# A hybrid recurrent decoder layer in fp32: the low half of each weight unit kept in HBM after its first use

## The chip, the cores and the metric

The kernel runs on one core of one Trainium2 chip. The metric is the device time of one execution in microseconds (us), lower is better. TensorE is called PE, VectorE DVE, ScalarE ACT and GpSimd POOL, as in the profile; SP is the engine whose queue issues every DMA of this kernel.

## The reference, cut to what matters

One layer over a prompt of 2048 tokens and 8 x 4 sample tokens, width 1024. The four weight matrices are multiplied with all tokens; between the first and the second stand four recurrent mixers that work through the tokens in chunks.

```python
u = x @ w_in                       # 1024 -> 3860, split among mixers A, B, C, D
y = concat(A(u), B(u), C(u), D(u)) # gated DeltaNet, Mamba-2 SSD, HGRN2, mLSTM: causal, with a state
h = LayerNorm(alpha * x + y @ w_out)
x = LayerNorm(alpha * h + relu(h @ w_up)**2 @ w_down)   # 1024 -> 4096 -> 1024
```

## The kernel before

The tokens are cut into NB = 4 blocks of 512; the 32 sample tokens ride along with block 0 in the projection and with block 2 behind it (544 columns then, in two pieces). Blocks 0 to 3 go through the projection (`do_P`, 31 column tiles of `w_in`), then each block through `w_out` (`do_W`) and the feed-forward part (`do_F`). The mixers run beside this as streams ("ma" for A, "mb" for B, C and D).

Every product is made in three passes to keep fp32 accuracy: a weight and an activation are each split into a high part, rounded to the matmul's format, and a low part, the rest; then hi x hi, lo x hi and hi x lo are accumulated in PSUM. A *unit* of weights is 1024 (or, for `w_dn`, 512) rows by 128 columns and is streamed in halves of [128, 4, 128] floats, 256 KB. The list `units` holds all 832 halves in the order of their use: 248 of `w_in` (62, four times), 64 of `w_out`, 256 of `w_up` and 264 of `w_dn`. 206 of them are distinct.

- `w_get(i)` loads half i into a `wraw` buffer (four of them).
- `w_split()` makes `whi` (ACT, sometimes DVE: `cpv`) and `wlo` = `wraw` - `whi` (`tt` on POOL or DVE, as `tvp` chooses). Four buffers each.
- `gemm` calls `w_pump()` ahead of half `cur`; the pump loads up to half cur+4 and splits up to half cur+2. A half is 4 x 3 matmuls, or twice as many for 544 columns.
- `w_first` and `w_rest` do the split of the first four halves in two steps.

The order on each engine is the order in which the program is written out. A planner (`_Run`) sets it: it carries a clock per engine with rough costs, and after each k step of a product (`R.tick()`) lets those steps of the mixers, evacuations and norms through whose inputs should be ready. `tvp` asks the same clocks whether POOL or DVE would be done first. So a step that is taken out of the program moves the place of others. All instructions run in order on their engine; SP's queue is one such order, for loads, stores and the mixers' transfers alike. Nearly all engine calls pass through one helper line (253), and all DMAs but a few through line 374, so the names of the tiles tell the instructions apart: `pd` is a product's PSUM tile, `g` an activation, `nb<-ud32d` a broadcast that the DeltaNet solve reads back from HBM, `UA` to `UD` the projected activations in HBM, `hTd` the normed input there.

Of the kernel before, what the change touches and what calls it, by code (L numbers as in the profile page):

```python
# [10 lines left out]
F32 = mybir.dt.float32  # L11
# [32 lines left out]
LATE_W = 5.0  # L44
# [262 lines left out]
def _dve_cost(fn, n, out, k):  # L307
    if fn in ("bn_stats", "tensor_reduce"):
        n = 1
        for x in k["in_"].shape[1:]:  # L310
            n *= x
    per = {"reciprocal": 0.00625, "tensor_tensor_scan": 0.00195, "tensor_copy": 0.00053}.get(fn, 0.00106)
    if fn == "tensor_scalar" and _sb(k["in0"]):
        per = 0.00053
    if fn == "bn_aggr":
        return 0.13
    return 0.06 + n * per + 0.06 * _ptrs(k, ("scalar", "scalar1", "scalar2"))
# [6 lines left out]
def _pool_cost(fn, n, out, k):  # L324
    return 0.25 + n * {"tensor_tensor": 0.00214, "tensor_scalar": 0.0012, "tensor_copy": 0.0036}.get(fn, 0.001)
# [20 lines left out]
def kernel(ctx: ExitStack, tc: tile.TileContext, t):  # L346
# [17 lines left out]
    drp = ctx.enter_context(tc.tile_pool(name="drp", bufs=1, space=DRAM))  # L364
# [5 lines left out]
    mult, add, sub = ALU.mult, ALU.add, ALU.subtract  # L370
    vmax, vmin = ALU.max, ALU.min

    def dma(out, in_):
        nc.sync.dma_start(out=out, in_=in_)
        R.cost("dma", 0.55, 2.5)
# [13 lines left out]
    def tt(out, a, b, op, eng=None):  # L389
        (eng or V).tensor_tensor(out=out, in0=a, in1=b, op=op)  # L390
# [10 lines left out]
    def tvp(n, late=0.0):  # L401
        now = max(R.clock["pe"], R.cur.ready)
        v = max(R.clock["dve"], now) + _dve_cost("tensor_tensor", n, None, {})
        g = max(R.clock["pool"], now) + _pool_cost("tensor_tensor", n, None, {})
        return G if g < max(v, R.clock["pe"] + late) else V

    def cpv(out, in_, n, late=0.0):
        now = max(R.clock["pe"], R.cur.ready)
        if max(R.clock["act"], now) + _act_cost("", n, None, {}) <= max(max(R.clock["dve"], now) + _dve_cost("tensor_copy", n, None, {}), R.clock["pe"] + late):
            cp(out, in_)  # L410
        else:
            V.tensor_copy(out, in_)
# [110 lines left out]
    units = []  # L523
    wst = {"nload": 0, "nsplit": 0, "cur": 0, "turn": 0}
    raws, his = {}, {}

    def w_get(i):
        w = sb4.tile([128, 4, 128], F32, tag="wraw", name="wraw")
        dma(w, units[i])
        raws[i] = w  # L530

    def w_pump():
        cur = wst["cur"]
        while wst["nload"] < min(cur + 5, len(units)):
            i = wst["nload"]
            w_get(i)
            wst["nload"] += 1
            if wst["nsplit"] < min(cur + 3, wst["nload"]):
                w_split()
        while wst["nsplit"] < min(cur + 3, len(units)):  # L540
            w_split()

    def w_split():
        i = wst["nsplit"]
        w = raws.pop(i)
        hi = sb4.tile([128, 4, 128], F32R, tag="whi", name="whi")
        lo = sb4.tile([128, 4, 128], F32R, tag="wlo", name="wlo")
        cpv(hi, w, 512, LATE_W - 1.0)
        tt(lo, w, hi.bitcast(F32), sub, tvp(512, LATE_W))
        his[i] = (hi, lo)  # L550
        wst["nsplit"] += 1

# [5 lines left out]

    def w_rest(i, eng):
        hi, lo = his[i]  # L560
        tt(lo, raws.pop(i), hi.bitcast(F32), sub, eng)

    def pieces(nt):
        if nt <= 512:
# [73 lines left out]
    def split_next(key):  # L638
        if not pend[key]:
            return  # L640
        k, st, nt = pend[key].popleft()
        XS[key].append(split_kt(st, k, nt))

    def queue_set(key, tiles, nt):
        pend[key] = deque((k, x, nt) for k, x in enumerate(tiles))
        XS[key] = []

    def fin_set(key):
        R.until(lambda: key in pend)
        while pend[key]:  # L650
            split_next(key)
        return XS.pop(key)
# [18 lines left out]
    def ln0_start():  # L671
# [5 lines left out]
        for src, n in tiles:  # L677
            x = [g2(), g2()]
            for half in range(2):
                dma(x[half][:n, 0:512], src[:, half * 512:half * 512 + 512])  # L680
            xs.append(x)
        w_get(0)
        dma(con, t["consts"])
        w_get(2)
        dma(par, t["params"])
        w_get(1)
# [11 lines left out]
        for i, half, e in ((1, 0, "a"), (2, 0, "g"), (4, 0, "v"), (3, 0, "a"), (0, 0, "g"), (0, 1, "v"), (4, 1, "v"), (1, 1, "a"), (2, 1, "g"), (3, 1, "v")):  # L698
# [5 lines left out]
            else:  # L704
                ts(xv, xv, r_, mult, m_, add, G if e == "g" else V)
        w_first(2)
        w_rest(0, G)
        w_rest(2, V)
        xs = xs[1:] + xs[:1]
        px = psa.tile([128, 512], F32, tag="a", name="pa_")  # L710
# [7 lines left out]
        def first(k):  # L718
            if k in (0, 1):
                w_first(2 * k + 1)  # L720
                w_rest(2 * k + 1, G)
            xh, xl = XS["P", 0][k]
            for u in range(2):
                hi, lo = his[2 * u + k // 4]
                seq = ((hi, xh), (lo, xh), (hi, xl))
                for n, (w, x) in enumerate(seq):
                    for p, c0, cn in psu[u]:
                        mm(p[:, 0:cn], w[:, k % 4, :], x[:, c0:c0 + cn], start=k == 0 and n == 0, stop=k == 7 and n == 2)

        for k in range(8):  # L730
# [17 lines left out]
            if k == 5:  # L748
                for i in range(4, 8):
                    w_get(i)  # L750
                wst["nload"] = 8
        w_split()
        w_split()
        setup()
# [48 lines left out]
    def y_pre(b):  # L803
# [5 lines left out]
        for k in range(8):  # L809
            st.append(load_kt(yTd[b], yTx, k, nt))  # L810
            yield
        queue_set(("W", b), st, nt)
        for k in range(EARLY_W):
            split_next(("W", b))
            yield
# [941 lines left out]
    def do_P(b, xs, nt):  # L1757
        for u in range(2 if b == 0 else 0, NPU):
            if b == NB - 1 and u == W0_AT:
                do_W(0, fin_set(("W", 0)), f_nt(0))  # L1760
                XS["F", 0] = {}
# [10 lines left out]
    def do_W(b, xs, nt):  # L1772
        acc = accs[b] = []
        st = deque(load_kt(hTd[b], hTx, d, nt) for d in range(2))
        for d in range(8):
            if d + 2 < 8:
                st.append(load_kt(hTd[b], hTx, d + 2, nt))
            ps = pieces(nt)
            gemm(ps, xs)
            acc.append(g2())  # L1780
            R.start(w_evac(ps, nt, acc[d], st.popleft()))
# [178 lines left out]
    def f_nt(b):  # L1960
        return NTM if b == FDEC else TB

    def do_F(b):
# [10 lines left out]
        for c in range(FFB):  # L1974
# [9 lines left out]
            elif b + 1 < NB:  # L1984
                do_W(b + 1, fin_set(("W", b + 1)), f_nt(b + 1))
                XS["F", b + 1] = {}
# [30 lines left out]
            del r2[c]  # L2017

    def fill_units():
        W = lambda: [units.extend([t["w_out_u"][d, 0], t["w_out_u"][d, 1]]) for d in range(8)]  # L2020
        for b in range(NB):
            for u in range(NPU):
                if b == NB - 1 and u == W0_AT:
                    W()
                units.extend([t["w_in_u"][u, 0], t["w_in_u"][u, 1]])
        for b in range(NB):
            f = 0
            for c in range(FFB):
                for j in range((4 if c == 0 else 3) + (1 if c + 1 < FFB else 0)):
                    units.extend([t["w_up_u"][f, 0], t["w_up_u"][f, 1]])  # L2030
                    f += 1
                if c == FFB - 1 and b + 1 < NB:
                    W()
                for q in range(2 if b == NB - 1 and c == FFB - 1 else 1):
                    units.extend(t["w_dn_u"][c, d] for d in range(8))

    fill_units()
    ln0_start()
    dma(lng, t["ln2_g"].partition_broadcast(128))
# [126 lines left out]
```

## Time and profile before

| | |
|---|---|
| median of 3 runs | 3067.88 us (3064.59 to 3075.63) |
| profiled execution | 3071.5 us, span 3069.7 us |
| busy: PE, DVE, ACT, POOL | 2897.1, 2156.1, 1244.2, 1632.5 us |
| granted TensorE clock, mean | 0.983 |
| DMA | 404.04 MB on SP's queue, 46.3% of the 16 DMA engines' time |

The span runs from the first to the last instruction. "Busy" counts an engine's own work, not waits. A row of a group gives the engine, the operation, out<-in, the count, then busy time and mean ns of one, then the idle time just ahead of it with what ended it. A row of waits gives total, number and longest. The stages by time: the projections of the four blocks up to about 1050 us, block 0's `w_out` inside their end; then `do_F` of block 0 up to about 1600, of blocks 1 to 3 up to the end. The mixers run from about 200 to 2420 us.

### The profile page before, as it was taken

Reading aid. Unit: us, or ns where it says so; the run is one execution under the profiler, and the core shown is the slowest. Engines: PE = TensorE matmul, PEld = TensorE weight load, DVE = VectorE, ACT = ScalarE, POOL = GpSimd, SP = SyncE. Lnnn points to the kernel's source line nnn. Section 1 sums busy time; section 2 is a strip of 40 time slices with the busy share of each in tenths; the row PEclk is TensorE's granted clock in tenths of the full one; section 3 lists DMA queues with packets and bytes.
Section 4 is the critical chain, followed back from the end, with each engine's and each line's share of the span. In section 5 each row is a group of like instructions: output and inputs, shape, how many; then the busy total and the mean of one; then the engine's idle time right before and its main releaser. Section 6 shows DMA issues by size and latency. Waiting matters only on the chain. (4 is left out here: it accounts for less than half of the span.)

```text
span 3069.7 us, 48033 instructions
## 1 busy us (share of the span) xinstructions
PE 2897.1 (94%) x16668; PEld 2479.8 (81%) x16668; DVE 2156.1 (70%) x4077; ACT 1244.2 (41%) x2653; POOL 1632.5 (53%) x1982
## 2 busy tenths in 40 slices
PE   7889899998999899999999999999999999999997
PEld 7778767777877778888787877778899999888886
DVE  6867887896986677777767865665887644474445
ACT  4554564564563533333244322233533222432222
POOL 5656664865664544554564536444363344444545
PEclk9999999999999999999999999999999999999998
DMA  6765465446556444454443435355343432333333
GB/s 188 85 186 166 121 190 164 130 129 201 121 159 192 139 120 124 132 173 119 138 145 115 144 91 139 118 159 153 92 147 105 125 93 84 112 120 93 99 95 98
DMA packets 361262, 407.10 MB, mean 133 GB/s; under 512 B 65468, under 2 KB 207804, under 8 KB 361020
## 3 DMA queue, kind: packets, MB, share of 16 engines
q1 hardware_dynamic: 361020, 404.04, 46.3%
q8 instruction: 132, 2.16, 0.3%
q14 instruction: 110, 0.90, 0.1%
HBM read 340.20 MB, written 63.72 MB: 132 GB/s over the span
## 5 line engine op out<-in xcount | busy, mean ns | idle before, releaser
L253 PE MATMUL pd<-g,whi 128*128 128x512 f32 (+2 forms) x8080 | 2242.6, 362 | 29.1 <-ACT g L253 17.2
L253 POOL TENSOR_TENSOR wlo<-wraw,whi 128x512 fp32r<-128x512 f32 x727 | 1031.8, 1426 | 1268.2 <-ACT whi L253 1071.8
L253 PEld LDWEIGHTS pd<-g,whi 128*128 128x128 f32 x8080 | 1393.6, 190 | 238.5 <-ACT g L253 19.4
L253 PE MATMUL pd<-g,wlo 128*128 128x512 f32 (+2 forms) x4040 | 1307.7, 355 | 16.4 <-POOL wlo L253 15.1
L253 PEld LDWEIGHTS pd<-g,wlo 128*128 128x128 f32 x4040 | 720.7, 190 | 113.2 <-POOL wlo L253 22.7
L253 ACT ACTIVATE whi<-wraw 128x512 fp32r<-128x512 f32 x797 | 489.2, 626 | 476.7 <-PE pd L253 256.0
L253 DVE TENSOR_TENSOR g<-g 128x512 fp32r<-128x512 f32 (+5 forms) x344 | 341.5, 995 | 157.2 <-ACT g L253 151.3
L253 ACT ACTIVATE g<-pd 128x512 f32<-128x512 f32 (+2 forms) x340 | 172.5, 526 | 473.7 <-PE pd L253 473.3
L253 DVE TENSOR_TENSOR g<-g,pd 128x512 f32<-128x512 f32 (+2 forms) x288 | 159.4, 570 | 211.7 <-PE pd L253 211.3
L253 ACT ACTIVATE g<-g 128x512 f32<-128x512 f32 (+4 forms) x350 | 212.9, 632 | 81.1 <-DVE g L253 40.1
L253 POOL TENSOR_TENSOR a<-nb,x 128x124 f32<-128x124 f32 (+30 forms) x496 | 198.4, 400 | 70.4 <-DMA nb<-ud32d 41.2
L253 POOL TENSOR_TENSOR x<-x,a 128x124 f32<-128x124 f32 (+30 forms) x496 | 199.5, 402 | 38.9
L253 DVE CAST g<-g 128x512 fp32r<-128x512 f32 (+1 forms) x162 | 158.4, 978 | 27.6 <-POOL g L253 21.2
L253 ACT ACTIVATE b<-b 128x256 f32<-128x256 f32 (+3 forms) x201 | 81.6, 406 | 182.2 <-DVE b L253 176.1
L253 DVE TENSOR_TENSOR wlo<-wraw,whi 128x512 fp32r<-128x512 f32 x105 | 83.1, 792 | 74.2 <-ACT whi L253 70.6
L253 DVE SCALAR_TENSOR_TENSOR g<-g 128x512 f32<-128x512 f32 (+3 forms) x124 | 117.8, 957 | 14.6 <-ACT g L253 14.2
L253 DVE SCALAR_TENSOR_TENSOR g<-g,par 128x512 f32<-128x512 f32 (+1 forms) x128 | 125.5, 998 | 0.1
L253 POOL TENSOR_TENSOR g<-g 128x512 f32<-128x512 f32 (+3 forms) x74 | 106.8, 1447 | 32.5 <-ACT g L253 25.1
L253 DVE TENSOR_TENSOR b<-laC 128x64 f32<-128x64 f32 (+3 forms) x466 | 110.2, 294 | 0.1
L253 DVE TENSOR_SCALAR g<-g 128x512 int32<-128x512 int32 (+6 forms) x137 | 79.7, 600 | 29.6 <-ACT g L253 28.7
L253 DVE TENSOR_TENSOR kzD<-laC,b 64x128 f32<-64x128 f32 (+1 forms) x228 | 98.6, 432 | 1.7
L253 DVE SCALAR_TENSOR_TENSOR g<-g,pd 128x512 f32<-128x512 f32 (+1 forms) x80 | 45.2, 581 | 67.0 <-PE pd L253 66.4
(2558 smaller groups left out, 2815.3 us busy)
## 6 DMA issues: line engine op xcount, KB each, us to landing
wraw<-in_w_dn_u_dram SPq DMA_DIRECT2D x264, 256.0 KB
wraw<-in_w_up_u_dram SPq DMA_DIRECT2D x256, 256.0 KB
wraw<-in_w_in_u_dram SPq DMA_DIRECT2D x248, 256.0 KB
nb<-ud32d SPq DMA_DIRECT2D x128, 256.0 KB
wraw<-in_w_out_u_dram SPq DMA_DIRECT2D x64, 256.0 KB
UC<-g SPq DMA_DIRECT2D x40, 256.0 KB
g<-in_x_prompt_dram SPq DMA_DIRECT2D x32, 256.0 KB
hTd<-g SPq DMA_DIRECT2D x32, 256.0 KB
```

The costliest lines, as they stand in the source:

```text
L253: r = f(*a, **k)
```

## The change

On the first use of a half that will be used again, the low part is computed as before and, two splits later, stored from its `wlo` tile to a DRAM tile of its own (`lod`). On each later use the low part isn't computed: the `wlo` tile is filled by a DMA from there. The high part is made by ACT at each use, from `wraw`, which is loaded each time as before. To know which halves are alike, `units` is filled through `need`, which gives each a key and counts its uses.

```diff
+    keys, uses, lod, kept = [], {}, {}, deque()
+
+    def need(key, ap):
+        keys.append(key)
+        uses[key] = uses.get(key, 0) + 1
+        units.append(ap)
+
...
+    def lo_make(i, lo, w, hi, eng):
+
+        key = keys[i]
+        if key in lod:
+            dma(lo.bitcast(F32), lod[key])
+            return
+        tt(lo, w, hi.bitcast(F32), sub, eng())
+        if uses[key] > 1:
+            lod[key] = drp.tile([128, 4, 128], F32, name=f"lod{len(lod)}")
+            kept.append((i, key, lo))
+
+    def lo_keep(n):
+        while kept and kept[0][0] <= n:
+            _, key, lo = kept.popleft()
+            dma(lod[key], lo.bitcast(F32))
...
     def w_split():
         i = wst["nsplit"]
         w = raws.pop(i)
+        lo_keep(i - 2)
         hi = sb4.tile([128, 4, 128], F32R, tag="whi", name="whi")
         lo = sb4.tile([128, 4, 128], F32R, tag="wlo", name="wlo")
         cpv(hi, w, 512, LATE_W - 1.0)
-        tt(lo, w, hi.bitcast(F32), sub, tvp(512, LATE_W))
+        lo_make(i, lo, w, hi, lambda: tvp(512, LATE_W))
...
     def w_rest(i, eng):
         hi, lo = his[i]
-        tt(lo, raws.pop(i), hi.bitcast(F32), sub, eng)
+        lo_make(i, lo, raws.pop(i), hi, lambda: eng)
...
     def fill_units():
-        W = lambda: [units.extend([t["w_out_u"][d, 0], t["w_out_u"][d, 1]]) for d in range(8)]
+        def half(name, u):
+            for k in range(2):
+                need((name, u, k), t[name][u, k])
+
+        W = lambda: [half("w_out_u", d) for d in range(8)]
...
-                for q in range(2 if b == NB - 1 and c == FFB - 1 else 1):
-                    units.extend(t["w_dn_u"][c, d] for d in range(8))
+                for q in range(2 if b == NB - 1 and c == FFB - 1 else 1):
+                    for d in range(8):
+                        need(("w_dn_u", c, d), t["w_dn_u"][c, d])
```

SP's queue in the projection of block 1, where the eight rows of the normed input of block 2 (`hTd_152`) are stored; before:

```order
L374 DMA wraw<-in_w_in_u_dram 128x512 x2
L374 DMA nb<-ud32d 128x1x512
L374 DMA hTd_152<-g 128x512 x8
L374 DMA wraw<-in_w_in_u_dram 128x512
L374 DMA UB_166<-g 128x4x128 x2
L374 DMA wraw<-in_w_in_u_dram 128x512
L374 DMA UB_166<-g 128x4x128 x2
L374 DMA nb<-ud32d 128x1x512
```

The same place after the change, with `lod` the kept low parts:

```order
L374 DMA wraw<-in_w_in_u_dram 128x512
L374 DMA wlo<-lod_1784 128x512
L374 DMA UA_165<-g 128x4x128
L374 DMA nb<-ud32d 128x1x512
L374 DMA hTd_152<-g 128x512 x8
L374 DMA wraw<-in_w_in_u_dram 128x512
L374 DMA wlo<-lod_1860 128x512
L374 DMA UA_165<-g 128x4x128
L374 DMA yTd_154<-b_4736 128x2x128
```

Each raw load now has the load of a low part behind it, in the same queue, and the mixers' transfers stand at other places.

POOL in the forward substitution of a DeltaNet chunk (`a` and `x` are its work tiles), before:

```order
L253 TENSOR_TENSOR x_108<-x_108,a_5852 128x4x12
L253 TENSOR_TENSOR wlo<-wraw,whi 128x512
L253 COPY g<-haloA_119 128x3
L253 TENSOR_TENSOR wlo<-wraw,whi 128x512
L253 TENSOR_TENSOR a_5852<-nb,x_108 128x4x11
L253 TENSOR_TENSOR x_108<-x_108,a_5852 128x4x11
```

Such a place after it:

```order
L253 TENSOR_TENSOR a_5998<-nb,x_108 128x4x3
L253 TENSOR_TENSOR x_108<-x_108,a_5998 128x4x3
L253 TENSOR_TENSOR a_5998<-nb,x_108 128x4x2
L253 TENSOR_TENSOR x_108<-x_108,a_5998 128x4x2
L253 TENSOR_TENSOR a_5998<-nb,x_108 128x4
L253 TENSOR_TENSOR x_108<-x_108,a_5998 128x4
```

From block 1 on the weight subtractions are gone from between POOL's steps.

SP's queue in the last block's feed-forward part, with what each DMA waits for (`DMAHW`: the landing of the DMA eight places ahead; an engine's name: the buffer or the data); before:

```order
L374 DMA wraw<-in_w_dn_u_dram 128x512 [waits DMAHW6_49,Pool_49]
L374 DMA wraw<-in_w_dn_u_dram 128x512 [waits DMAHW7_49,Pool_49]
L374 DMA wraw<-in_w_dn_u_dram 128x512 [waits DMAHW0_49,Pool_49]
L374 DMA wraw<-in_w_dn_u_dram 128x512 [waits DMAHW1_49,Pool_49]
L374 DMA wraw<-in_w_dn_u_dram 128x512 [waits DMAHW2_49,Pool_49]
```

After it:

```order
L374 DMA wlo<-lod_16278 128x512 [waits DMAHW3_49,PE_49]
L374 DMA wraw<-in_w_dn_u_dram 128x512 [waits DMAHW4_49,Activation_49]
L374 DMA wlo<-lod_16334 128x512 [waits DMAHW5_49,PE_49]
L374 DMA wraw<-in_w_dn_u_dram 128x512 [waits DMAHW6_49,Activation_49]
L374 DMA wlo<-lod_16392 128x512 [waits DMAHW7_49,PE_49]
L374 DMA wraw<-in_w_dn_u_dram 128x512 [waits DMAHW0_49,Activation_49]
```

A raw load's buffer is now free when ACT has read it, and a low part's when PE has done its last matmul with the half four places back.

More of the change, by code (lines that the diff above doesn't have):

```diff
@@ L2024, in fill_units @@
                     W()
-                units.extend([t["w_in_u"][u, 0], t["w_in_u"][u, 1]])
+                half("w_in_u", u)
         for b in range(NB):
@@ L2029, in fill_units @@
                 for j in range((4 if c == 0 else 3) + (1 if c + 1 < FFB else 0)):
-                    units.extend([t["w_up_u"][f, 0], t["w_up_u"][f, 1]])
+                    half("w_up_u", f)
                     f += 1
```

## The prediction

> **What bounds the kernel now.** I read the page's shares, then the busy time by stage, then the waits, then single places in the timeline. The page first, and the core's mean clock:
>
> ```profile
> PE 2897.1 (94%) x16668; PEld 2479.8 (81%) x16668; DVE 2156.1 (70%) x4077; ACT 1244.2 (41%) x2653; POOL 1632.5 (53%) x1982
> q1 hardware_dynamic: 361020, 404.04, 46.3%
> core 0: 3069.7 us, clock 0.983
> ```
>
> TensorE is busy 2897.1 of 3069.7 us. Its work stays as it is, so the change can move only the 172.6 us of PE idle time and the clock: (1 - 0.983) x 3069.7 = 52 us are lost at half clock. The same by stage, the first and last 20 to 30 us left out:
>
> ```profile
> core 0: us, PE busy (x) PEld busy (x) DVE busy (x) ACT busy (x) POOL busy (x), PEclk, DMA share, GB/s
> 20.00:265.00 245.00, 216.40 (x1623) 211.91 (x1624) 181.11 (x325) 131.78 (x294) 150.54 (x149) 0.97 0.69 153
> 265.00:1050.00 785.00, 725.40 (x3539) 581.06 (x3537) 635.10 (x1154) 429.68 (x892) 479.15 (x594) 0.98 0.54 156
> 1050.00:1580.00 530.00, 510.50 (x2662) 421.68 (x2663) 385.33 (x809) 189.98 (x441) 271.02 (x410) 0.98 0.46 136
> 1580.00:2230.00 650.00, 624.74 (x3693) 522.05 (x3693) 463.46 (x1006) 233.47 (x517) 319.90 (x458) 0.99 0.43 126
> 2230.00:2700.00 470.00, 463.83 (x3508) 449.95 (x3507) 278.37 (x513) 149.45 (x320) 216.77 (x203) 1.00 0.37 110
> 2700.00:3040.00 340.00, 337.06 (x1520) 276.61 (x1519) 177.90 (x193) 94.58 (x165) 171.00 (x126) 0.99 0.36 103
> ```
>
> Stage length minus PE busy gives 28.6, 59.6, 19.5, 25.3, 6.2 and 2.9 us of PE idle time, 142 in all: this is the most that any relief can bring. It lies in the projection blocks (up to 1050), where DVE is 81% busy and the DMA share is highest.
>
> **The change part by part.**
>
> *Removed.* The program has 832 halves of weight units, 206 of them distinct; 626 low parts are no longer computed (in the built programs `wlo` goes from 727 to 166 on POOL and from 105 to 40 on DVE). What they cost:
>
> ```profile
> L253 POOL TENSOR_TENSOR wlo<-wraw,whi 128x512 fp32r<-128x512 f32 x727 | 1031.8, 1426 | 1268.2 <-ACT whi L253 1071.8
> L253 DVE TENSOR_TENSOR wlo<-wraw,whi 128x512 fp32r<-128x512 f32 x105 | 83.1, 792 | 74.2 <-ACT whi L253 70.6 <-ACT dnD L253 2.3 <-POOL x L253 1.0
> PE pd L253 <- POOL wlo L253: 15.1, 19, 1.9
> ```
>
> So 561 x 1.426 = 800 us leave POOL and 65 x 0.792 = 51 us leave DVE. POOL is 53% busy and hardly ever what PE waits for: 15.1 us in 19 waits. That 15.1 is the sure gain. Less sure: POOL stands 1071.8 us in front of a `wlo` subtraction until ACT has made `whi`, with the mixers' work queued behind it; without that, DVE and POOL steps of the mixers come earlier, and some of the other 142 - 15 = 127 us of PE idle time goes. Its bounds are 0 and 127; I take a quarter, 32, because the waits in the projection blocks end on DVE and ACT, whose own work (DVE 51 of 2156 us) hardly shrinks. Gain in idle time: 15 + 32 = 47 us.
>
> *Added: 626 loads and 206 stores of 256 KB on SP's one queue.* The page's queue line prices one: 46.3% of 3069.7 us over 404.04 MB is 3.52 us per MB, so 0.262 MB takes 0.92 us of all 16 DMA engines. How many units each stage has, by who made the low part:
>
> ```profile
> 265.00:1050.00 785.00, 324.52 (x810) 155.28 (x808) 31.68 (x37) 252.97 (x167) 0.98 0.54 156
> 1560.00:2230.00 670.00, 264.38 (x759) 137.70 (x758) 21.51 (x28) 185.78 (x137) 0.99 0.44 127
> 2230.00:3040.00 810.00, 422.81 (x1543) 260.62 (x1542) 4.19 (x6) 353.45 (x260) 1.00 0.37 107
> ```
>
> The last two counts are DVE and POOL: 204 (16 of them W_out, first used there, so 188 loads), 165 and 266. At 0.92 us each the DMA share rises by 0.22, 0.23 and 0.30, to 0.76, 0.67 and 0.67: no saturation on average, but PE now waits for a transfer that is issued just in time. The load of half i is emitted at the pump of half i-2, behind the raw load of i+2, and its buffer is free only when PE is done with i-4. A half lasts 785/204 = 3.8 us in the projections and 810/266 = 3.0 us late. The window from issue to need is then two halves, 7.7 us, where SP stands at the program's place. The raw load has the same two halves until ACT wants it, so ACT's waits for raw loads show what such a window is worth:
>
> ```profile
> ACT whi L253 <- DMA wraw<-in_w_in_u_dram: 33.3, 18, 4.8
> ACT whi L253 <- DMA wraw<-in_w_out_u_dram: 1.5, 1, 1.5
> ...
> ACT whi L253 <- DMA wraw<-in_w_up_u_dram: 27.9, 10, 6.5
> ACT whi L253 <- DMA wraw<-in_w_dn_u_dram: 12.2, 5, 4.6
> ACT whi L253 <- DMA wraw<-in_w_out_u_dram: 11.4, 3, 5.5
> ...
> ACT whi L253 <- DMA wraw<-in_w_up_u_dram: 16.4, 7, 5.2
> ACT whi L253 <- DMA wraw<-in_w_dn_u_dram: 6.9, 3, 3.6
> ACT whi L253 <- DMA wraw<-in_w_out_u_dram: 0.9, 1, 0.9
> ```
>
> These are the stretches 265 to 1050, 1580 to 2230 and 2230 to 3040: 34.8, 51.5 and 24.2 us, in 19, 18 and 11 waits of some 2.3 us. They cost PE nothing now, since ACT is ahead of it. One such place, SP first and ACT behind it:
>
> ```profile
> 427.09 0.53 SPq L374 DMA_DIRECT2D nb<-ud32d  x1
> 427.67 6.64 SPq L374 DMA_DIRECT2D hTd<-g  x8
> 434.73 0.33 SPq L374 DMA_DIRECT2D wraw<-in_w_in_u_dram  x1
> 439.82 0.63 ACT L253 ACTIVATE whi<-wraw 128x512 fp32r<-128x512 f32 x1 [4.19 <-DMA wraw<-in_w_in_u_dram]
> ```
>
> Eight stores of `hTd` behind an `nb` broadcast hold SP for 6.6 us, and the raw load issued behind them is used only 5.1 us after its issue. The changed kernel keeps this row of eight with an `nb` ahead of it and has a `wlo` load right behind. If lateness grows with the DMA share, the three sums become 34.8 x 0.76/0.54 = 49, 51.5 x 0.67/0.43 = 80 and 24.2 x 0.67/0.37 = 44: 173 us. Bounds of what reaches PE: nothing, if SP stands ahead of the program's place by as much as the loads are late, and all 173. I take half, 86: late loads come in clusters, in which one stall makes room for the next. The 206 stores fall into the stretches of first use, 20 to 265 and 1050 to 1560, where ACT waits for raw loads as follows:
>
> ```profile
> ACT whi L253 <- DMA wraw<-in_w_in_u_dram: 13.0, 8, 4.1
> ...
> ACT whi L253 <- DMA wraw<-in_w_up_u_dram: 20.5, 8, 5.9
> ACT whi L253 <- DMA wraw<-in_w_dn_u_dram: 19.6, 7, 4.3
> ACT whi L253 <- DMA wraw<-in_w_out_u_dram: 3.1, 1, 3.1
> ```
>
> 56 us; a fifth more of it (the DMA share there rises by about 0.2), and half of that on PE, is 5 us.
>
> *Moved.* SP's queue changes its releasers:
>
> ```profile
> SPq L374 <- POOL wlo L253: 918.7, 389, 10.6
> SPq L374 <- DVE b L253: 328.2, 86, 14.8
> ```
>
> The 918.7 us for POOL (raw buffer free) become waits for ACT's `whi`, which is earlier, but each `wlo` load holds the queue until PE has left half i-4, with raw loads, `nb`, `laC` and all stores behind it. That ties SP to within about one half of PE's place (3 to 4 us); the waits for mixers' stores, up to 14.8 us, then delay the next `wlo` load. This is inside the 173. SP has time to issue: 832 more at 0.33 us are 275 us.
>
> *Clock.* A gap on PE costs more than itself:
>
> ```profile
> 456.00:459.00 3.00, 0.62 (x6) 0.51 (x5) 3.00 (x7) 2.44 (x6) 1.80 (x3) 1.00 0.47 102
> 459.00:463.00 4.00, 4.00 (x16) 3.24 (x16) 3.95 (x12) 1.98 (x4) 1.88 (x2) 0.61 1.02 313
> ```
>
> After 2.4 us of idle time the granted clock is 0.61 for 4 us, 1.6 us lost. Over the program 52 us lost stand to 172.6 us idle, so I multiply idle time by 1.30. The Trainium skill ("TensorE: Matmul & The Clock Gate", section "Why this matters for your kernels") asks only that no gap be longer than about 3 us; by it stalls of 2.3 us would cost no clock, and the sum would be 86 + 5 - 47 = 44 us. The rows show a dip after a shorter gap, so here the measurement decides.
>
> *Sum.* (86 + 5 - 47) x 1.30 = 57 us. The profiled execution took 3071.5 us (span 3069.7 plus 1.8 around it); the median of the runs is 3067.88, 3.6 lower. 3071.5 + 57 - 3.6 = 3125 us.
>
> **The rivals.**
>
> *A. Faster: the freed POOL pays and the loads stay hidden.* Place: the projections and mixers up to 2230. For it speaks how long DVE's subtractions take beside POOL's work:
>
> ```profile
> L253 DVE TENSOR_TENSOR g<-g 128x512 fp32r<-128x512 f32 x156 | 166.9, 1073 | 21.2 <-ACT g L253 17.0
> L253 DVE TENSOR_TENSOR wlo<-wraw,whi x105: 670/694/1773, 17.5 to 2261.8; 128x512 fp32r<-128x512 f32 x105
> ```
>
> The same shape takes 670 ns at best and 1073 on the mean, so 156 x 0.4 = 63 us of DVE time in this group alone is waiting inside the instruction; with 51 us of removed work that is 114 us of DVE. If this halves the other idle time, the gain is (15 + 64) x 1.30 = 103; with a quarter of the 173 late us reaching PE, 56: 3068 - 47 = 3021 us. It decides when less than a quarter or so of the lateness reaches PE (47 of 173 us cancel my own gain). The Trainium skill ("SBUF — State Buffer", section "SBUF: two separate sides") states the mechanism: a DVE operation with two SBUF inputs and a GpSimd operation exclude each other for the whole instruction. The spread of the rows agrees with it. Against A: these DVE groups are waited for by PE in only part of 127 us.
>
> *B. No change.* PE stays the bound, loss and gain cancel (47 us each): 3068 us. For it: the late stretch from 2700 has 2.9 us of idle time, and a window of 8 us for a load.
>
> *C. Much slower: all of the lateness reaches PE.* In the program each DMA also waits for the landing of the one eight places ahead in SP's queue, so a slow landing holds the issue of later loads; with two transfers per half those eight are four halves or fewer instead of eight. Then 3068 + (173 + 5 - 47) x 1.30 = 3238 us. Against it: mean shares stay under 0.8.
>
> **How the numbers follow.** Forecast (slower, 3085 to 3165): 0.50. A: 0.20. B: 0.17. C: 0.13. Predicted 3125. The range leaves out the lower half of A (under 3035) and most of C (over 3190). The forecast and C give slower 0.63, B gives 0.17, A gives 0.20; half a percent, 15 us, is about what a measurement of this kernel tells from no change.
>
> **What would show it.** Right: PE waits for `DMA wlo<-lod` in the two stretches up to 2230, several tens of us, most behind `nb`, `hTd` or groups of stores; more short clock dips; POOL near 830 us busy; DMA shares near 0.76 and 0.67; an unchanged stretch from 2700. Wrong: PE idle below 172 us with few waits for `lod` (A), or late loads in the quiet last stage as well (C). The gain term is wrong if the mixers' waits on DVE and ACT do not change.

## The result and the profile after

The changed kernel takes 3091.45 us (median of 4 runs, 3088.9 to 3094.0) against 3071.41 us for the kernel before in the same comparison (4 runs): ratio 1.0067, 95% interval 1.0043 to 1.0091. It is slower by 20 us, where 57 were forecast. The direction and the range held; the size did not.

The page's busy line and queue line, and the core's clock, of the changed kernel (profiled execution 3088.9 us):

```profile
PE 2891.7 (94%) x16668; PEld 2485.4 (81%) x16668; DVE 1773.7 (57%) x3997; ACT 1258.0 (41%) x2664; POOL 847.1 (27%) x1437
q1 hardware_dynamic: 480828, 622.20, 67.2%
```

```profile
core 0: 3087.1 us, clock 0.980
```

POOL fell by 785 us, as forecast (847 against some 830). VectorE fell by 382 us, which was not: 51 us of subtractions left it. PE's idle time rose from 172.6 to 3087.1 - 2891.7 = 195.4 us. By stage (columns as before):

```profile
core 0: us, PE busy (x) PEld busy (x) DVE busy (x) ACT busy (x) POOL busy (x), PEclk, DMA share, GB/s
20.00:265.00 245.00, 199.54 (x1441) 194.11 (x1442) 160.85 (x282) 123.68 (x275) 126.35 (x118) 0.92 0.82 197
265.00:1050.00 785.00, 725.05 (x3657) 596.84 (x3657) 512.71 (x1221) 423.59 (x890) 256.52 (x483) 0.97 0.76 228
1050.00:1580.00 530.00, 505.36 (x2666) 415.73 (x2666) 383.83 (x811) 201.12 (x453) 251.02 (x402) 1.00 0.66 203
1580.00:2230.00 650.00, 618.35 (x3549) 512.25 (x3548) 362.76 (x959) 232.20 (x515) 159.59 (x361) 0.98 0.63 192
2230.00:2700.00 470.00, 466.73 (x3583) 455.72 (x3583) 196.64 (x444) 153.30 (x318) 20.35 (x23) 1.00 0.59 185
2700.00:3040.00 340.00, 340.00 (x1522) 277.83 (x1521) 117.89 (x191) 101.93 (x175) 14.93 (x10) 1.00 0.63 193
```

Stage length minus PE busy is now 45.5, 60.0, 24.6, 31.7, 3.3 and 0 us, against 28.6, 59.6, 19.5, 25.3, 6.2 and 2.9. The first stage, where stores and the moved order are all that is new, lost 17 us; the kernels e1 and e8 below put most of that to the stores (33.2 us of PE idle time there without added traffic, 47.5 with the stores). From 1050 to 1580, where halves of `w_out`, `w_up` and `w_dn` have their first use, POOL still subtracts and is about as busy as before (251 against 271 us). The projections look unchanged, but their waits are others. The waits (total, number, longest):

```profile
PE pd L253 <- DMA wlo<-lod: 60.4, 26, 8.3
POOL a L253 <- DMA nb<-ud32d: 424.2, 78, 44.8
POOL wlo L253 <- DMA lod<-wlo: 37.2, 11, 13.5
ACT whi L253 <- DMA wraw<-in_w_in_u_dram: 74.4, 27, 10.9
ACT whi L253 <- DMA wraw<-in_w_out_u_dram: 40.2, 16, 5.7
```

One of these rows misleads by itself. POOL waited for the broadcasts as follows before, and in e1 below, which has no added traffic:

```profile
POOL a L253 <- DMA nb<-ud32d: 41.2, 22, 4.4
```

```profile
POOL a L253 <- DMA nb<-ud32d: 338.8, 62, 44.9
```

Most of the rise from 41.2 to 424.2 us is thus no sign of late broadcasts: POOL, with its subtractions gone, stands where it used to work.

SP's own waits, its largest row:

```profile
SPq L374 <- PE pd L253: 643.1, 402, 5.4
```

PE waits 60.4 us for loads of low parts. Of that, 42 us lie in the projections and 15 from 1580 to 2230. PE's other waits fell from 59 to 17 us in the projections and from 25 to 17 in the later stretch. Summed over PE's rows for 265 to 1050, waits for DVE's `b` tiles fell from 19.3 to 2.2 us, those for ACT's `g` from 10.9 to 4.5. `SPq <- PE pd`, new and the queue's largest wait, is each load held until PE has left the buffer.

The longest of PE's waits, in the projection of block 3. First SP's queue, then PE, then stretches with the clock in the column ahead of the DMA share:

```profile
899.58 1.86 SPq L374 DMA_DIRECT2D b<-RB  x3
901.49 0.59 SPq L374 DMA_DIRECT2D b<-UD  x1
905.48 0.34 SPq L374 DMA_DIRECT2D wraw<-in_w_in_u_dram  x1
906.53 0.32 SPq L374 DMA_DIRECT2D wlo<-lod  x1
...
912.57 0.79 PE L253 MATMUL pd<-g,wlo 128*128 128x512 f32 x1 [8.26 <-DMA wlo<-lod]
```

```profile
903.50:912.50 9.00, 0.81 (x4) 0.32 (x2) 1.03 (x2) 1.50 (x3) 2.66 (x8) 0.69 0.79 162
912.50:917.00 4.50, 4.43 (x11) 3.46 (x11) 3.17 (x5) 0.00 (x0) 0.00 (x0) 0.50 1.04 269
```

SP issues a mixer's operands until 902.1, stands until 905.48, and the low part issued at 906.53 reaches PE 6.0 us later, after 8.3 us of idle time; half clock for 4.5 us follows. This is the picture that the prediction drew. It is not where most of the loss is.

The gain, in the groups of like instructions (busy time, mean ns of one):

```profile
L253 POOL TENSOR_TENSOR wlo<-wraw,whi 128x512 fp32r<-128x512 f32 x166 | 232.5, 1406 | 373.0 <-ACT whi L253 288.8 <-DMA lod<-wlo 37.2 <-DMA b<-RB 11.6
L253 DVE TENSOR_TENSOR g<-g 128x512 fp32r<-128x512 f32 x156 | 120.7, 778 | 30.5 <-ACT g L253 25.7
L253 DVE CAST g<-g 128x512 fp32r<-128x512 f32 x122 | 73.3, 601 | 14.1 <-POOL g L253 9.6 <-ACT g L253 1.4
```

The same 156 subtractions on VectorE took 1073 ns each before and take 778 now. The casts take 601 ns, and took 944 before:

```profile
L253 DVE CAST g<-g 128x512 fp32r<-128x512 f32 x120 | 113.3, 944 | 18.9 <-POOL g L253 13.7 <-ACT g L253 2.3
```

### The profile page after: what moved, and what is told of

Its sections match the earlier page's. It is cut to its first block, busy times and chain, and to the rows that moved or that the text cites. A ratio compares the mean times of both kernels' runs of the same rounds, so it can differ in the third digit from the quotient of the medians.

```text
span 3087.1 us, 48361 instructions
## 1 busy us (share of the span) xinstructions
PE 2891.7 (94%) x16668; PEld 2485.4 (81%) x16668; DVE 1773.7 (57%) x3997; ACT 1258.0 (41%) x2664; POOL 847.1 (27%) x1437
## 4 chain that ended last, share of the span: by engine, by line
PE 61%; DMA 19%; DVE 8%; ACT 4%; POOL 3%; issue 3%; SPq 2%; POOLq 0%; DVEq 0%; ACTq 0%
PE pd L253 51%; DMA nb<-ud32d 5%; DMA wlo<-lod 4%; DVE g L253 4%; DMA lod<-wlo 3%; ACT g L253 2%; SPq L374 1%; DVE b L253 1%; DMA wraw<-in_w_in_u_dram 1%; POOL a L253 1%; DMA wraw<-in_w_out_u_dram 1%; POOL x L253 1%; DVE a L253 1%; POOL wlo L253 1%; DMA laC<-UC 1%
## 5 line engine op out<-in xcount | busy, mean ns | idle before, releaser
L253 PE MATMUL pd<-g,wlo 128*128 128x512 f32 (+2 forms) x4040 | 1310.7, 355 | 74.2 <-DMA wlo<-lod 60.4
L253 DVE TENSOR_TENSOR g<-g 128x512 fp32r<-128x512 f32 (+5 forms) x345 | 261.5, 762 | 317.9 <-ACT g L253 311.4
L253 POOL TENSOR_TENSOR wlo<-wraw,whi 128x512 fp32r<-128x512 f32 x166 | 232.5, 1406 | 373.0 <-ACT whi L253 288.8
L253 POOL TENSOR_TENSOR a<-nb,x 128x124 f32<-128x124 f32 (+30 forms) x496 | 183.6, 370 | 532.5 <-DMA nb<-ud32d 424.2
L253 POOL TENSOR_TENSOR g<-g,lng 128x512 f32<-128x512 f32 x17 | 25.8, 1516 | 357.7 <-ACT g L253 357.7
L253 DVE TENSOR_SCALAR g<-g 128x512 int32<-128x512 int32 (+6 forms) x137 | 63.9, 485 | 82.0 <-ACT g L253 80.9
L253 DVE SCALAR_TENSOR_TENSOR g<-g,par 128x512 f32<-128x512 f32 (+1 forms) x128 | 106.7, 841 | 5.6 <-ACT g L253 5.2
L253 DVE SCALAR_TENSOR_TENSOR g<-g 128x512 f32<-128x512 f32 (+3 forms) x124 | 97.2, 788 | 7.2 <-ACT g L253 6.9
L253 DVE CAST g<-g 128x512 fp32r<-128x512 f32 (+1 forms) x161 | 90.5, 562 | 17.1 <-POOL g L253 9.6
L253 DVE TENSOR_TENSOR b<-laC 128x64 f32<-128x64 f32 (+2 forms) x469 | 93.1, 258 | 4.7 <-DMA laC<-UC 4.7
L253 DVE TENSOR_TENSOR kzD<-laC,b 64x128 f32<-64x128 f32 (+1 forms) x228 | 82.3, 361 | 1.8
```

Source lines behind the costliest of these rows:

```text
L253: r = f(*a, **k)
```

## The experiments

Thirteen kernels, in four comparisons; each ratio is to runs of the kernel before in the same comparison, whose medians were 3071.4 (e1 to e6), 3073.2 (e7 to e10), 3078.6 (e11 to e13) and 3072.7 us (e14, e15). "Order of before" and "of after" say which planner charges a kernel keeps: with these, every instruction other than those of the low parts stands in that kernel's sequence on each engine. Only e3 has an order of its own. Diffs are cut to what matters.

| kernel | order | median us | ratio | 95% interval |
|---|---|---|---|---|
| no low parts on later uses, no traffic (e1b) | before | 2958.2 | 0.9633 | 0.9608 to 0.9658 |
| the same (e1) | after | 2982.4 | 0.9710 | 0.9684 to 0.9737 |
| the same with the 206 stores (e8) | after | 3008.3 | 0.9794 | 0.9778 to 0.9810 |
| stores, loads of a quarter of the bytes, unread (e7) | after | 3021.9 | 0.9839 | 0.9815 to 0.9862 |
| stores and whole loads, unread (e6) | after | 3076.1 | 1.0004 | 0.9985 to 1.0023 |
| the change | after | 3091.5 | 1.0067 | 1.0043 to 1.0091 |
| the change, loads a half earlier (e3) | its own | 3102.9 | 1.0097 | 1.0075 to 1.0119 |
| the change (e9) | before | 3074.5 | 1.0002 | 0.9985 to 1.0020 |
| the change for every second half (e10) | before | 3070.7 | 0.9997 | 0.9981 to 1.0014 |
| all computed, PE waits for none of later uses (e11) | before | 3075.1 | 0.9991 | 0.9977 to 1.0005 |
| the same, later subtractions a 16th as wide (e14) | before | 2961.7 | 0.9640 | 0.9623 to 0.9658 |
| all computed, later uses on VectorE (e12) | before | 3035.6 | 0.9861 | 0.9845 to 0.9877 |
| all computed, all but four halves on VectorE (e15) | before | 3015.2 | 0.9812 | 0.9789 to 0.9834 |
| every second half loaded, the rest on VectorE (e13) | before | 3054.2 | 0.9927 | 0.9912 to 0.9943 |

### The parts of the change, one by one

**e1b**: on later uses the low part is neither computed nor loaded, and the planner is charged as before. PE multiplies the high part a second time in its place, so PE's work is the same and the result lacks those products.

```diff
         if key in lod:
-            dma(lo.bitcast(F32), lod[key])
-            return
+            en = eng()
+            R.cost(en._name, en._cost("tensor_tensor", 512, None, {}), 0.15, True)
+            return hi
```

> Leaves out: on later uses of a weight half the low part is neither computed nor loaded, TensorE multiplies the high part a second time in its place; nothing is stored. All instructions that are left stand in the order of the kernel before. It measures what the removed 626 subtractions are worth by themselves. Theory 1 (the freed POOL and DVE bring the mixers' steps earlier, about 50 us of PE idle time): 3015 to 3035 us, PE idle near 115 us instead of 173. Rival (the fewer waits on DVE and ACT in the changed kernel come from the moved order of the instructions, not from the freed engines): 3055 to 3070 us, only the 15 us of waits for POOL's wlo gone.

**e1**: the same, charged as the changed kernel is (`R.cost("dma", 0.55, 2.5)` for each load and store).

> Leaves out the same, but with all instructions that are left in the order of the changed kernel, and no low part stored. Theory 1: 3015 to 3035 us, within 10 us of the run with the order of before. Rival (moved order): 3010 to 3025 us while the run with the order of before stays over 3055.

The removed subtractions are worth 113 us (e1b), almost twice the 61 of my sum, and both runs are faster than any range that I had set for them. The moved order takes 24 us of it back: e1 is slower than e1b and the intervals are apart. I had priced it at nothing. With the order, the planner's choice of engine moved too: in e1 24 more steps of the norms (128x512, the products with `lng` and the sums with `lnb`) run on POOL, which is busy for 863.2 us against 818.6 in e1b. How much of the 24 us is this and how much the order was not tried apart.

**e6**: the order, stores and loads of the changed kernel, but `lo_make` returns `hi` after issuing the load, so no matmul waits for one.

> The changed kernel's order, stores and loads of low parts, all issued; but on later uses TensorE multiplies the high part twice and reads no loaded low part (left out of the result), so PE never waits for these loads and SP's queue isn't held by PE. Theory 1 (the loss is PE's wait for late low parts, 60 us, and some 17 us from the stores in block 0): 3030 to 3045 us, 15 to 20 over the run without transfers in the same order. Rival 2 (the added traffic delays raw loads and the mixers' loads, and the waits for low parts are only where that shows): 3070 us or more. DMA share 0.76 in the projections in both.

It takes 94 us more than e1, and PE waits for no load of a low part: the traffic by itself brings this loss. PE's waits for these loads, and SP's queue held until PE has left a buffer, add the last 15 us, from 3076 to 3091. The waits of e6:

```profile
POOL a L253 <- DMA nb<-ud32d: 479.2, 81, 45.5
ACT whi L253 <- DMA wraw<-in_w_in_u_dram: 124.0, 41, 10.7
ACT whi L253 <- DMA wraw<-in_w_up_u_dram: 83.0, 34, 7.2
ACT whi L253 <- DMA wraw<-in_w_out_u_dram: 67.8, 28, 5.7
```

and of its queue on SP:

```profile
SPq L374 <- DMA nb<-ud32d: 203.4, 82, 4.5
```

What was PE's wait for low parts is spread over other waits. ACT's three rows are 74.4, 53.2 and 40.2 us in the changed kernel and 70.5, 37.7 and 12.4 in e1; POOL's row is 338.8 in e1 and SP's 45.5. PE's own waits from 20 to 2230 us are 84.8 us in e1 and 157.2 in e6; the largest rise is at VectorE's `a` tiles, which belong to the DeltaNet mixer (7.2 to 36.3 us). ACT waits longer for raw loads in e6 than in the changed kernel, so the two losses are not independent: 94 and 15 us hold for taking the parts away in this order. Late in the program, with few mixer steps left and then none, the traffic costs nothing; the last two stages of e6:

```profile
2230.00:2700.00 470.00, 468.42 (x3586) 458.70 (x3585) 195.78 (x436) 152.78 (x315) 19.09 (x17) 0.99 0.57 186
2700.00:3040.00 340.00, 340.00 (x1512) 277.61 (x1511) 114.79 (x185) 99.51 (x173) 14.94 (x10) 1.00 0.59 194
```

**e3**: the whole change, each load issued one half earlier, into one of five `wlo` buffers. To make room there are three `wraw` buffers instead of four, which is a second difference.

```diff
+    def lo_get(i):
+        if i < len(units) and i not in got and keys[i] in lod:
+            got.add(i)
+            los[i] = lop.tile([128, 4, 128], F32R, tag="wlo", name="wlo")
+            dma(los[i].bitcast(F32), lod[keys[i]])
...
             wst["nload"] += 1
+            lo_get(cur + 3)
```

> The whole computation. The load of a low part is issued one half earlier (at the pump of i-3), with five wlo buffers and three wraw buffers instead of four and four; buffer coupling to PE unchanged. Theory 1 (waits of 2.3 us on the mean, one half is 3.0 to 3.9 us): two thirds of the 60 us go, 3045 to 3060 us, below the changed kernel's 3091 and perhaps below the kernel before. Rival 2 (traffic): 3080 to 3095 us, the waits only move to raw loads.

```profile
PE pd L253 <- DMA wlo<-lod: 20.0, 13, 6.0
POOL a L253 <- DMA nb<-ud32d: 434.1, 79, 33.0
DVE b L253 <- DMA laC<-UC: 14.0, 7, 5.2
PE pb__3099 L253 <- DMA laC<-UC: 7.9, 1, 7.9
```

PE's wait for loads fell from 60.4 to 20.0 us, and the kernel did not become faster: 3102.9 us, above both ranges, the rival's being nearer. ACT's waits for raw loads are longer, 305 us against 203 in the changed kernel. Whether the earlier low parts, the missing raw buffer or the kernel's own order (VectorE has 3990 instructions, not 3997) makes them so was not tried apart.

**e8** leaves out the loads of e6 and keeps the stores; **e7** keeps all of its DMAs but makes each load a quarter as large (against e6):

```diff
-            dma(lo.bitcast(F32), lod[key])
+            dma(lo.bitcast(F32)[:, 0:1], lod[key][:, 0:1])
             return hi
```

> As the kernel without low parts on later uses and without their traffic (2982 us, order of after), but with the 206 stores. Theory (every transfer of 256 KB costs alike): 2982 + 94 x 206/832 = 3005 us. Rival (the stores lie in the stretches of first use, where few mixers run beside them, and cost nothing): 2982 us, within 7.

> As the kernel with all stores and loads in which PE reads the high part twice and does not wait for the loads (3076 us; low parts of later uses left out of the products), but each load brings a quarter of its bytes (64 KB): the count of DMAs and their places in SP's queue stay, 123 of 164 MB of loads go. Theory (the 16 DMA engines' bytes delay the other transfers): of the 94 us that the traffic costs over 2982 us, the stores have 206/832 = 23 us, the loads 71, of which a quarter is left, 18: 2982 + 23 + 18 = 3023 us, 3005 to 3040. Rival (the count: 626 more places in SP's one queue, whose waits and landings hold the transfers behind them): 3076 us, 3062 to 3084.

Both theories were met within 4 us. The stores cost 26 us, 0.126 us each. The 626 quarter loads cost 14 us over that, the whole ones 68: a fifth of the price for a quarter of the bytes at the same count and the same places in the queue. So for the loads the bytes decide, not SP's places. For the stores this is open: POOL also stands until a store has left its buffer (`POOL wlo <- DMA lod<-wlo`, 37.2 us in the changed kernel), and no run takes that apart. What the bytes do can be read from issue to landing, medians in us between 1100 and 2300 (and after 2300 in the last column):

| kernel | `nb` broadcast | raw `w_up` half | raw `w_up`, after 2300 |
|---|---|---|---|
| e1, no traffic | 6.6 | 4.1 | 2.6 |
| e8, stores | 7.0 | 4.4 | 2.6 |
| e7, quarter loads | 7.1 | 4.5 | 2.7 |
| e6, whole loads | 8.0 | 5.5 | 2.8 |
| before | 6.4 | 3.8 | 2.6 |
| the change | 7.7 | 5.2 | 2.9 |

A broadcast, of which there are 128, lands 1.3 us later with the whole traffic (the change against before), and the DeltaNet steps wait for them one after another; in the quiet stage a raw load of `w_up` is late by 0.1 to 0.3 us.

### The change without the moved order, and half of it

**e9**: the whole change; the planner is charged for a subtraction, as in e1b, and the added DMAs are issued without its charge (`nc.sync.dma_start`).

> The whole change (206 stores, 626 loads, PE reads the loaded low part), but the planner is charged for each low part as in the kernel before, so that every other instruction stands where it stood before the change. Theory: the moved order costs by itself, and its price without any traffic (2982 - 2958 = 24 us) adds to the rest: 3091 - 24 = 3067 us, 3058 to 3076, no difference from before. Rival: the price of the moved order exists only where PE waits for nothing else; beside the traffic both orders end at the same time: 3085 to 3097 us.

3074.5 us, no difference from before: the moved order costs 17 us beside the traffic too, 20 by the ratios (the intervals of e9 and of the change are apart). So in the order of before, what the change saves and what its traffic costs cancel, and that it is slower at all comes from the moved order. Which of the moved steps costs it stays open; PE's waits for loads are not it, since they are longer here:

```profile
PE pd L253 <- DMA wlo<-lod: 73.8, 34, 6.6
```

**e10**: e9, for the odd halves only (`if uses[key] > 1 and key[-1] % 2:`).

> The change made for every second half of the weights only (those whose last index is odd), the others computed at each use; order of before. Theory (transfers delay one another more than in proportion as the DMA share rises, the gain of the removed work is in proportion): half of the 113 us gain, 56, against less than half of the loss of 94 + 15, some 30: 3071 - 56 + 30 = 3045 us, 3030 to 3058. Rival (loss in proportion to the traffic): 3071 - 56 + 54 = 3069 us, no difference from before.

My theory fell, and the rival was right: half of the change is worth as little as all of it. Gain and loss in proportion would give this; the run shows only that they cancel, not each by itself.

### Where the 113 us come from

**e11**: the kernel before, with PE reading the high part twice on later uses. All subtractions are made; PE waits for none of the later ones, and the result lacks their low parts. Against e1b:

```diff
         if key in lod:
             en = eng()
-            R.cost(en._name, en._cost("tensor_tensor", 512, None, {}), 0.15, True)
+            tt(lo, w, hi.bitcast(F32), sub, en)
             return hi
```

> The kernel before with every low part computed at every use, but PE reads the high part twice on later uses and does not wait for the subtraction (low parts of later uses left out of the products); order of before. It splits the 113 us that the removed subtractions are worth. Theory (my sure term: PE's own waits for POOL's low parts, 15 us x 1.3 = 20; the other 93 come from POOL and DVE being free): 3072 - 20 = 3052 us, 3042 to 3062. Rival 1 (the waits are all of it): below 2980 us. Rival 2 (a wait for POOL only hides another wait that ends at the same time): 3072 us, no difference from before.

No difference: the 15.1 us that the prediction called sure were worth nothing that could be measured (the interval reaches from 7 us faster to 2 us slower). Rival 2 was right.

**e14**: e11, with each later subtraction on 32 of its 512 columns (`lo[:, :, 0:8]`, `w[:, :, 0:8]`, `hi[:, :, 0:8]`), on the same engine.

> The kernel before, order of before, no reuse; PE reads the high part twice on later uses and does not wait for the subtraction, and each later subtraction, on POOL or VectorE as before, works on 32 of its 512 columns only (low parts of later uses left out of the products). Each engine still stands in front of it until the high part is made. Theory (POOL's working time and what it does to VectorE's instructions is what the 113 us are): near the kernel without the subtractions, 2958 us: 2955 to 2990 us. Rival (POOL's queue: the mixers' steps stand behind a subtraction that waits for the high part, 1072 us of standing before): near the kernel with whole subtractions, 3055 to 3075 us.

2961.7 us, as fast as with no subtraction at all. The groups of e14:

```profile
L545 POOL TENSOR_TENSOR wlo<-wraw,whi 128x32 fp32r<-128x32 f32 x559 | 188.5, 338 | 1460.6 <-ACT whi L253 1328.0 <-issue 66.0 <-DVE whi L253 9.0
L253 DVE TENSOR_TENSOR g<-g 128x512 fp32r<-128x512 f32 x156 | 128.5, 827 | 29.7 <-ACT g L253 25.4
L253 DVE CAST g<-g 128x512 fp32r<-128x512 f32 x120 | 68.8, 573 | 14.6 <-POOL g L253 10.1 <-ACT g L253 1.5
```

POOL still stands 1328 us in front of a subtraction until ACT has made `whi`, longer than the 1072 us before, and that costs nothing. What costs is the subtractions' working time: with most of it gone, VectorE's groups are nearly as short as in e1b, whose busy line and groups are:

```profile
PE 2857.2 (97%) x16668; PEld 2467.7 (84%) x16668; DVE 1754.4 (59%) x4010; ACT 1240.2 (42%) x2653; POOL 818.6 (28%) x1423
```

```profile
L253 DVE TENSOR_TENSOR g<-g 128x512 fp32r<-128x512 f32 x156 | 127.1, 818 | 30.1 <-ACT g L253 25.7
L253 DVE TENSOR_TENSOR wlo<-wraw,whi 128x512 fp32r<-128x512 f32 x38 | 29.7, 785 | 38.8 <-ACT whi L253 38.7
```

VectorE's time without its own weight subtractions was 2156.1 - 83.1 = 2073 us before and is 1754.4 - 29.7 = 1725 us in e1b, with the same other instructions in the same order. So 559 POOL subtractions of 1.43 us, 797 us of POOL, lengthened VectorE's other work by 348 us. In e14 they are still 188 us of POOL, in short pieces, and VectorE's other work is 1789.6 - 28.6 - 17.0 = 1744 us, only 19 us longer than in e1b.

Two things are to be added. First, e1b and e14 also take 67 subtractions off VectorE. That is the smaller part: e12 below has 626 of them on VectorE and is 70 us slower than e1b by the ratios, so an estimate for 67 is 7 or 8 of the 113 us. Second, a shorter subtraction on POOL also lets the mixers' steps behind it on POOL start earlier. How the gain divides between this and the shorter instructions on VectorE was not tried apart.

**e12** computes everything and moves the later subtractions to VectorE, in the places that they had; **e15** moves all but the first four halves' (`if i > 3:` in place of `if key in lod:`). Against e1b:

```diff
             en = eng()
             R.cost(en._name, en._cost("tensor_tensor", 512, None, {}), 0.15, True)
-            return hi
+            nc.vector.tensor_tensor(out=lo, in0=w, in1=hi.bitcast(F32), op=sub)
+            return lo
```

> The whole computation without reuse: every low part computed at every use, but on later uses always on VectorE (559 subtractions moved from POOL); order of before; no added DMA. Theory (what the removal frees is POOL: its queue, which stands in front of a subtraction, and the VectorE instructions that POOL lengthens): VectorE goes from 1774 us busy without the subtractions to some 2200 (626 x 0.7 us more), about as much as before, and part of the 113 us is kept: 3035 us, 3010 to 3060. Rival (the mixers' waits on VectorE set the end; 390 us of work moved to it make them longer): 3095 us or more, slower than before.

> The whole computation without reuse: all subtractions but the first four on VectorE, those of the first uses too; order of before; no added DMA. Theory (each subtraction moved from POOL to VectorE is worth 43 us / 559 = 0.077 us): 165 more, 3036 - 13 = 3023 us, 3014 to 3031. Rival (in the stretches of first use, 20 to 265 us above all, VectorE has no room, 74% busy there and PE waiting for nothing of POOL's but a few us): no faster than 3036 us.

Both theories held (3035.6 and 3015.2 us). Both kernels are faster than the kernel before, by 1.4 and 1.9%, and than the changed one, without a byte of added traffic. The page and the groups of e15:

```profile
PE 2872.5 (95%) x16668; PEld 2467.7 (82%) x16668; DVE 2153.5 (71%) x4801; ACT 1243.2 (41%) x2653; POOL 648.9 (22%) x1258
```

```profile
L545 DVE TENSOR_TENSOR wlo<-wraw,whi 128x512 fp32r<-128x512 f32 x828 | 598.9, 726 | 377.1 <-ACT whi L253 362.4 <-DMA UB<-g 3.5 <-ACT dnD L253 2.5
L253 DVE TENSOR_TENSOR g<-g 128x512 fp32r<-128x512 f32 x156 | 111.7, 719 | 11.9 <-ACT g L253 7.6
```

VectorE makes 828 subtractions (599 us) and is busy for 2153.5 us, as long as before with 105 of them: what it takes over, it gets back from shorter instructions. POOL is left with 649 of 1632 us.

**e13** loads every second half (e9) and computes the other on VectorE (e12).

> The whole computation: on later uses every second half's low part is loaded (313 loads, 103 stores), the other half's is computed on VectorE, none on POOL; order of before. Theory (traffic costs in proportion, half of 109 = 55; POOL is free as in the full change): 3072 - 113 + 55 + some 20 for 313 subtractions on VectorE = 3034 us, 3015 to 3052: faster than both kernels. Rival (what is gained goes with the number of subtractions removed, on whichever engine they are): 3072 us, as when every second half was loaded and the others stayed on POOL.

3054 us. By the ratios it is some 21 us faster than e10, where the other halves stayed mostly on POOL, but 20 us slower than my theory and just outside its range, and slower than e12, which loads nothing.

## Why the prediction was right in direction, by luck, and wrong in size

Measured against the terms of the sum, all in us of the kernel's time:

| step | forecast | measured | by |
|---|---|---|---|
| PE's own waits for POOL's low parts | 15 x 1.3 = 20 gain | about 3, within noise | e11 |
| the other gain | 32 x 1.3 = 42 | about 110 | e1b less e11 |
| moved order | 0 | 24 loss (17 beside the traffic) | e1 less e1b; change less e9 |
| stores | 5 x 1.3 = 6.5 loss | 26 | e8 less e1 |
| loads, as traffic | none beside PE's wait | 68 | e6 less e8 |
| loads, as PE's wait | 86 x 1.3 = 112 loss | 15 | change less e6 |
| sum | +57 | -113 + 24 + 26 + 68 + 15 = +20 | |

- *The direction was luck.* The sum set a gain of 61 against a loss of 118 us. They measured 113 and 109 and nearly cancel, as e9 shows directly (ratio 1.0002). This is rival B's picture, at nearly twice its size. The 20 us by which the change is slower come from the moved order, which the sum did not have, and without which the time would have been outside the stated range.
- *The gain term is the step that failed, in size and in mechanism.* "A quarter of the other idle time" rested on POOL's standing in front of subtractions and on VectorE's own work hardly shrinking. The standing costs nothing (e14), and VectorE shrank by 382 us; PE's idle time fell by 75 us from before to e1b, not by 47. The row that said so was quoted under rival A: 1073 ns on the mean against 670 at best. I priced it for one group, 63 us; summed over VectorE's groups it is 348. Rival A's gain of 103 us was near the 113; its loss of 56 was too small.
- *The term that I called sure was the one worth nothing.* A wait's row tells what ended it last, not what would have ended it otherwise.
- *The loss came out near, 109 us against 118, by another way.* PE's wait was forecast to be nearly all of it; with that wait taken away, 94 of 109 us remained. Lateness had been read from ACT's waits for raw loads as if only the new loads could carry it to PE. It reaches PE through other transfers as well, the mixers' and the raw loads (e6); by which steps was read from waits, not tried one by one. "Late loads come in clusters" thus gave about the right number for a wrong reason.
- *The moved order was left out.* The listing showed that mixers' transfers stand at other places; no price was put on it, and it cost about as much as the whole difference.
- *The multiplier* of 1.30 was low: from e1 to e6 PE's idle time goes from 115.5 to 189.4 us and the span by 102 us, 1.38; from before to e1b they go from 172.6 to 97.6 and the span by 114.9, 1.53.
- *Right:* the DMA shares (0.76 from 265 to 1050 and 0.63 from 1580 to 2230, against 0.76 and 0.67), POOL's busy time, where PE waits for loads (57 of 60.4 us in the two stretches), what stands ahead of them in SP's queue (at each of these waits of 1 us or more, mixers' transfers or `hTd` stores are among the nine DMAs ahead of the load), and the last stage, unharmed at a DMA share of 0.63. Clock dips hardly became more: 22 against 21, and the mean clock went from 0.983 to 0.980.

## What to carry to other kernels

A kept intermediate that is loaded again can delay, by its bytes, the transfers of the streams that run beside it: here 626 loads and 206 stores cost 109 us, as much as the work that they replaced was worth, while the bound engine waited only 60 us for the loads by name. Before work is taken off an engine that is not the bound, look at how much longer the other engines' instructions are beside it than alone; moving that work, at no bytes, may bring more than avoiding it. Where a planner sets the order, hold the order fixed in one experiment, since a removed step moves all others and that has a price of its own.

## What the hardware showed that I had not expected

A wait on POOL costs nothing that could be measured (1328 us of it in e14, which is as fast as e1b), and 1.43 us of POOL's work costs VectorE's other instructions 0.62 us on the mean (348 us over 559). The Trainium skill ("SBUF — State Buffer", section "SBUF: two separate sides") says that a VectorE instruction in a two-port mode, or one with two SBUF inputs beside a POOL instruction that reads SBUF, and the POOL instruction exclude each other for the whole instruction. The trace agrees in that the two-input subtractions became shorter (1073 to 818 ns in e1b); the one-input casts became shorter as well (944 ns before, 573 in e14), and no run here tells in which mode they run.

The price of a transfer's bytes depends on who runs beside it. From 2420 to 3040 us, where no mixer is left, the changed kernel has 213 loads at a DMA share of 0.61 and PE idle for 0.0 us (2.9 before). Ahead of 2230, at 0.63 to 0.82, the same kind of load, with the stores, delayed a broadcast by 1.3 us on the median.
